# A float32 two-block transformer on one core: where the context stream's low parts are made, how many raw weight buffers it has, and in which order four matmul strips stand

## The chip, the cores and the metric

One core of a Trainium2 chip. The metric is the device time of one execution in microseconds; medians of several runs are compared. The core has five engines, which run their own instruction queues in order and wait for each other by semaphores: TensorE (PE; its weight loads are shown as PEld), VectorE (DVE), ScalarE (ACT), GpSimd (POOL) and SyncE (SP), which here issues all large DMAs.

## The reference

Two blocks after each other, all in float32, on 256 tokens of width 1024. Cut to what matters here:

```python
def first_block(x, ...):                  # "block 1"
    proj = rms_norm(x) @ w_in             # RWKV-7 columns and sparse-attention columns
    y_r = rwkv7_group(proj[..., :R_COLS], ...)   # a scan over 256 tokens, 8 heads
    y_n = nsa_group(proj[..., R_COLS:], ...)     # three kinds of attention
    h = x + concat([y_r, y_n]) @ w_out
    h = h + swiglu(rms_norm(h), ...)
    return rms_norm(h)

def second_block(x, c, ctx, c_ctx, ...):  # two layers
    for l in range(2):
        mod_x = silu(c) @ w_ada[l] + b_ada[l]        # 9216 columns, one row
        mod_c = silu(c_ctx) @ w_ada[l] + b_ada[l]    # the same weights, a second row
        h_x = half_ffn(h_x, mod_x[0:3]); h_c = half_ffn(h_c, mod_c[0:3])
        # mixer (neighbourhood attention, pooling, grouped attention), out projection, second half_ffn
    return rms_norm(h_x)
```

`h_c`, the context stream, starts from `ctx` and not from block 1, so its first feed-forward can run beside block 1.

## The kernel before, in words

A float32 product is made from three fast ones: each operand is split into a high part (rounded to the fast format) and a low part (what is left), and high x high, low x high and high x low are summed in PSUM. For the weights this is `Stream.get` (L351 to L358): a tile of 512 KB is loaded into a raw buffer (`r`, L349), ScalarE casts it to the high part (`h`, L356), and the stream's engine `self.e` subtracts to make the low part (`l`, L357). `gemm` (L360) then issues, for eight slices k, the products with `h` (L364, L365), and after them those with `l` (L368). Three numbers set a stream's depth: `nr` raw buffers and `nh` of each part.

Three streams matter. `st` in `block1` (L549, 2 raw buffers, 3 of each part) feeds block 1's projection: eight tiles in its first loop (L578 to L583), then 17 tiles of which 15 are L631's loop, then eight compression weights that are loaded raw; the first two of these go to the raw buffers and the other six straight into part buffers (L347). `st_c` (L1595, 3 raw buffers, 2 of each part, low parts on GpSimd) feeds the context stream: its feed-forward (66 tiles) and its mixer (14 tiles). `st_c` also carries the modulation weights, which are only loaded (L1162) and used raw. A third stream `s` feeds everything else, on VectorE.

The modulation (`Ada.step`, L1155) multiplies two rows (padded to 32) with 2048 columns at a time: four strips of 512 columns, which go to four groups of 32 PSUM partitions (L1168), eight slices k each. The strips of one k lie in two raw tiles, two strips each. The last part of a layer has strips of 256 columns, all four in one tile. 80 such quartets are made in all: 43 ahead of block 1's output projection, the rest during the feed-forwards of the second block's first layer.

The order of the work on each engine is set by a scheduler, which simulates the engines and picks, of the instructions that could run, the earliest in program order. Block 1 stands ahead of the context stream in the program, so the context's matmuls (output tiles `f`, inputs `yhc`, `ylc`, `hh`, `hl`) fill what block 1 leaves. The end of block 1, the RWKV part, is serial:
- Gram matrices (L951), a round trip through DRAM, 31 steps of two VectorE operations each that invert small triangles (L977, L978), a second round trip, and the products with the result (L994 to L1007);
- the chunk loop: for each of eight chunks of 32 tokens L1023, an addition on VectorE (L1024), L1031 and L1032, and an update of the state on VectorE (L1041);
- the tail: L1048, L1064, L849 with a power on GpSimd (L855), L864, L1083 and L1084, then block 1's output projection, whose first matmul is L364 with input `mixh`, at 530.70 us.

Of the kernel before, what the change touches and what calls it, by code (L numbers as in the profile page):

```python
# [15 lines left out]
OP = mybir.AluOpType  # L16
AX = mybir.AxisListType
PSUM = bass.MemoryType.PSUM
DRAM = bass.MemoryType.DRAM

D = 1024
KD = 8
# [243 lines left out]
def build(tc, A, O, dbg=(), stop=None):  # L266
    nc = tc.nc
    v, s, g, te, sy = nc.vector, nc.scalar, nc.gpsimd, nc.tensor, nc.sync
    es = ExitStack()
# [29 lines left out]
    f32 = lambda a: a.bitcast(F32)  # L299
# [31 lines left out]


    class Stream:
        def __init__(self, name, nr, nh, side=None, stack=es, eng=None, parts=None):
            self.nr = nr
            self.raw = pool(name + "r", nr, side=side, stack=stack)
            self.h = pool(name + "h", nh, side=side, stack=parts or stack)
            self.l = pool(name + "l", nh, side=side, stack=parts or stack)
            self.q = sy
            self.e = eng or v  # L340

        def load(self, src, a, b, i=0):

# [8 lines left out]
        def get(self, src, a, b):  # L352
            r = self.load(src, a, b)
            h = tl(self.h, [128, 1024], F32R, tag="h")[:, 0:a * b].rearrange("p (a b) -> p a b", a=a)
            l = tl(self.l, [128, 1024], F32R, tag="l")[:, 0:a * b].rearrange("p (a b) -> p a b", a=a)
            s.copy(h, r)  # L356
            self.e.tensor_tensor(l, r, f32(h), op=OP.subtract)  # L357
            return h, l  # L358

    def gemm(pt, w, m0, m1, xs):  # L360
# [126 lines left out]
    def block1(ps, early, ready):  # L487
# [12 lines left out]
        with tc.tile_pool(name="ropet", bufs=1) as rp:  # L500
# [8 lines left out]
            for i, ph in ((0, 0.25), (1, 0.0)):  # L509
# [4 lines left out]
                r = tl(rp, [128, 24], name="r")  # L514
# [31 lines left out]
            next(early, None)  # L546
        with ExitStack() as e:
            yp = pool("b1y", 1, stack=e)
            st = Stream("s1", 2, 3, stack=e)  # L549
            yh = tl(yp, [128, KD, T], F32R, name="yh")  # L550
            yl = tl(yp, [128, KD, T], F32R, name="yl")
            with ExitStack() as e2:
# [17 lines left out]
            for b in range(2):  # L570
                pts = [ps(512), ps(512)]
                for kp in range(4):
                    wh, wl = st.get(A["w1m"][b, kp], 2, 512)
                    for k2 in range(2):
                        k = kp * 2 + k2
# [4 lines left out]
                    for k2 in range(2):  # L580
                        k = kp * 2 + k2
                        for t in range(2):
                            te.matmul(pts[t], yh[:, k, t * 128:t * 128 + 128], wl[:, k2], start=False, stop=k == KD - 1)  # L583
                for t in range(2):
                    cos, sin = rope[:, 0, t * 8:t * 8 + 8], rope[:, 1, t * 8:t * 8 + 8]
                    if b == 0:
                        q = tl(pp, [128, 8, 64], tag="qtm", bufs=1)
# [5 lines left out]
                        for h4 in range(2):  # L593
                            pt = ps(512)
# [8 lines left out]
                    else:  # L603
# [8 lines left out]
                        pt = ps(512)  # L612
# [18 lines left out]
            for m in range(15):  # L631
                w = st.get(A["w1s"][m], 8, 128)
# [3 lines left out]
                pt = ps(T)  # L636
# [8 lines left out]
                nr = 32 if m == 14 else 128  # L645
# [17 lines left out]
            for i, (pe, nm) in enumerate((("pe_k", "k"), ("pe_v", "v"))):  # L663
                w = st.get(A["w1s"][15 + i], 8, 128)
                pt = ps(T)
# [57 lines left out]
        with ExitStack() as e:  # L723
            pp = pool("nsap", 2, stack=e)
            pcT = [None, None]
            for t in range(2):
                psc = ps(128)
                for h in range(8):
                    q = QT[:, h, t * 128:t * 128 + 128]
# [4 lines left out]
                sc = tl(pp, sh, tag="csc")  # L734
# [11 lines left out]
                pt = ps(128)  # L746
# [3 lines left out]
            for t in range(2):  # L750
                nk = 128 * (t + 1)
                po = ps(512, tag="o")
                for pr in range(4):
                    PT = []
                    for h in (2 * pr, 2 * pr + 1):
                        kv = h // 4
                        q = QT[:, h, t * 128:t * 128 + 128]
# [26 lines left out]
                    for b in range(nb + 1):  # L784
                        for j in range(2):
                            h = 2 * pr + j
                            out = po[j * 64:j * 64 + 64, pr * 128:pr * 128 + 128]
                            if b < nb:
                                w, kt = divmod(b, t + 1)
# [15 lines left out]
        with ExitStack() as e:  # L805
# [183 lines left out]
            for t in range(2):  # L989
                pw = ps(512)  # L990
                for p in range(4):
                    for j in range(2):
                        h = 2 * p + j
# [17 lines left out]
            for t in range(2):  # L1011
                py = ps(512, tag="o") if t == 0 else ps(512, tag="o")
                pyv = py.rearrange("p (a i) -> p a i", a=4)
                for q in range(4):
# [12 lines left out]
                    if c < 7:  # L1027
                        pS = ps(512)
                        for p in range(4):
                            w = slice(p * 128, p * 128 + 128)  # L1030
# [12 lines left out]
                for p in range(4):  # L1043
                    for b in range(2):
                        for j in range(2):
                            h = 2 * p + j
# [95 lines left out]
    class Ada:  # L1142
# [12 lines left out]
        def step(self, i, st, ps):  # L1155
            l, M = self.l, self.M
            src = A[f"ada{l}"]
            n = 512 if i < 4 else 256
            pt = ps(n)
            for k in range(KD):  # L1160
                if i < 4:
                    ws = [st.load(src[i * 16 + k * 2 + b].rearrange("p (a b) -> p a b", a=2), 2, 512) for b in range(2)]  # L1162
                    w = [ws[j // 2][:, j % 2] for j in range(4)]
                else:
                    ws = st.load(src[64 + k].rearrange("p (a b) -> p a b", a=4), 4, 256)
                    w = [ws[:, j] for j in range(4)]
                for j in range(4):
                    te.matmul(pt[j * 32:j * 32 + 32], adac[:, k], w[j], start=k == 0, stop=k == KD - 1)  # L1168
                if k < KD - 1:
                    yield  # L1170
            y = tl(st.pad, [128, 512], tag="ada", bufs=1)[:, 0:n]
            s.copy(y, pt)
            p2 = ps(n)
            nb = n // 128
            for b in range(nb):
                te.transpose(p2[:, b * 128:b * 128 + 128], y[:, b * 128:b * 128 + 128], ident)
            m = self.M_[:, i * 16:i * 16 + 4 * nb]
            v.tensor_copy(m.rearrange("p (j b) i -> p j b i", j=4), p2.rearrange("p (b j c) -> p j b c", b=nb, j=4)[:, :, :, 0:2])
            v.tensor_add(m, m, V(f"bada{l}")[:, i * 16:i * 16 + 4 * nb, None].to_broadcast([128, 4 * nb, 2]))
            gg = V(f"ng{l}").rearrange("p (j k) -> p j k", j=3)  # L1180
            for m in ((0, 1), (2, 3), (4, 5), (6, 7), (8,))[i]:
                if m % 3 == 1:
                    v.scalar_tensor_tensor(self.GS[:, m // 3], M[:, m], 1.0, gg[:, m // 3, :, None].to_broadcast([128, 8, 2]),
                                           op0=OP.add, op1=OP.mult)
                elif m in (2, 8):
                    v.tensor_scalar(M[:, m], M[:, m], 0.5, None, op0=OP.mult)
            yield
# [404 lines left out]

    rs, rs2 = ExitStack(), ExitStack()
    pad = pool("pada", 1, side=R, stack=rs)
    st_c = Stream("sc", 3, 2, side=R, stack=rs, eng=g, parts=rs2)  # L1595
    st_c.pad = pad
    e = ExitStack()
    first = []
# [165 lines left out]
```

## Time and profile before

| | us |
|---|---|
| median of 3 runs | 2322.16 |
| lowest, highest | 2317.82, 2325.53 |
| the profiled execution | 2317.79 |
| its span, first to last instruction | 2315.6 |
| TensorE busy in it | 2215.6 |
| VectorE, ScalarE, GpSimd busy | 1365.0, 965.7, 361.1 |

How to read it: the span is the profiled execution's own; what lies between it and 2317.79 us is around the first and the last instruction. Busy is the time in which an engine has an instruction in work. An engine's idle time matters only where another engine, on the path to the end, waits for it. In the rows below, "L1168" is a line of the kernel, `f<-r,sc` names the output and input tiles, and an arrow `<-` behind a time in brackets names what ended a wait.

### The profile page before, as it was taken

Reading aid. Unit: us, or ns where it says so; the run is one execution under the profiler, and the core shown is the slowest. Engines: PE = TensorE matmul, PEld = TensorE weight load, DVE = VectorE, ACT = ScalarE, POOL = GpSimd, SP = SyncE. Lnnn points to the kernel's source line nnn. Section 1 sums busy time; section 2 is a strip of 40 time slices with the busy share of each in tenths; the row PEclk is TensorE's granted clock in tenths of the full one; section 3 lists DMA queues with packets and bytes.
Section 4 is the critical chain, followed back from the end, with each engine's and each line's share of the span. In section 5 each row is a group of like instructions: output and inputs, shape, how many; then the busy total and the mean of one; then the engine's idle time right before and its main releaser. Section 6 shows DMA issues by size and latency. Waiting matters only on the chain.

```text
span 2315.6 us, 38336 instructions
## 1 busy us (share of the span) xinstructions
PE 2215.6 (96%) x15317; PEld 1935.3 (84%) x15317; DVE 1365.0 (59%) x2442; ACT 965.7 (42%) x1602; POOL 361.1 (16%) x286
## 2 busy tenths in 40 slices
PE   7999988998999899998999999999999999989998
PEld 3687876878999799997878777798888889878998
DVE  4465567348665876667765333357534347776665
ACT  4334432226444555445643222245332325564443
POOL 2025464444010300002010000011000002310000
PEclk9999999999999999999999999999999999999999
DMA  8765544436655245554166434376623235413554
GB/s 312 255 220 191 175 159 143 135 121 215 197 183 176 91 129 167 185 168 144 58 221 228 175 131 167 134 236 210 200 87 97 95 119 170 140 46 122 187 183 127
DMA packets 114929, 376.25 MB, mean 162 GB/s; under 512 B 18464, under 2 KB 24480, under 8 KB 114752
## 3 DMA queue, kind: packets, MB, share of 16 engines
q1 hardware_dynamic: 114752, 373.82, 49.1%
q8 instruction: 120, 1.97, 0.3%
q14 instruction: 57, 0.47, 0.1%
HBM read 372.20 MB, written 1.57 MB: 161 GB/s over the span
## 4 chain that ended last, share of the span: by engine, by line
PE 76%; issue 9%; DVE 7%; DMA 4%; POOL 2%; ACT 1%; SPq 0%; POOLq 0%; DVEq 0%; ACTq 0%
PE m L364 13%; PE m L365 13%; PE m L368 13%; PE f L364 8%; PE f L365 7%; PE f L368 7%; PE f L1168 4%; PE o L1399 2%; DVE l L357 1%; PE f L1389 1%; DMA r<-in_up 1%; ACT h L356 1%; DMA r<-in_ada 1%; DVE tm L977 1%; POOL sa L400 1%
## 5 line engine op out<-in xcount | busy, mean ns | idle before, releaser
L356 ACT CAST h<-r 128x1024 fp32r<-128x1024 f32 (+1 forms) x547 | 570.0, 1043 | 950.4 <-PE m L365 453.9
L357 DVE TENSOR_TENSOR l<-r,h 128x1024 fp32r<-128x1024 f32 (+1 forms) x467 | 575.5, 1233 | 284.1 <-ACT h L356 236.7
L365 PE MATMUL m<-yl,h 128*128 128x256 f32 (+1 forms) x1624 | 441.9, 303 | 3.5 <-DVE yl L437 3.4
L364 PE MATMUL m<-yh,h 128*128 128x256 f32 (+1 forms) x1624 | 441.5, 303 | 1.5 <-ACT yh L436 1.5
L364 PEld LDWEIGHTS m<-yh,h 128*128 128x128 f32 x1624 | 310.1, 192 | 27.3 <-issue 10.4
L365 PEld LDWEIGHTS m<-yl,h 128*128 128x128 f32 x1624 | 310.4, 192 | 21.4 <-DVE yl L437 6.4
L368 PE MATMUL m<-yh,l 128*128 128x256 f32 (+1 forms) x1624 | 258.6, 300 | 0.0
L357 POOL TENSOR_TENSOR l<-r,h 128x1024 fp32r<-128x1024 f32 x80 | 194.2, 2431 | 368.2 <-ACT h L356 234.3
L368 PEld LDWEIGHTS m<-yh,l 128*128 128x128 f32 x1624 | 225.1, 190 | 14.2 <-issue 3.7
L400 POOL TENSOR_TENSOR sa<-sa,sq 128x256 f32<-128x256 f32 x81 | 83.3, 1029 | 873.2 <-ACT sq L396 462.9
L365 PE MATMUL m<-hl,h 128*128 128x256 f32 (+1 forms) x738 | 207.0, 303 | 0.0
L364 PE MATMUL m<-hh,h 128*128 128x256 f32 (+1 forms) x738 | 197.2, 304 | 0.0
L364 PE MATMUL f<-yh,h 128*128 128x256 f32 (+1 forms) x624 | 185.3, 321 | 1.1 <-ACT yh L436 1.1
L365 PE MATMUL f<-yl,h 128*128 128x256 f32 (+1 forms) x624 | 184.1, 319 | 0.0
L365 PEld LDWEIGHTS m<-hl,h 128*128 128x128 f32 x738 | 139.8, 189 | 6.9 <-issue 0.4
L364 PEld LDWEIGHTS m<-hh,h 128*128 128x128 f32 x738 | 135.9, 189 | 11.1 <-issue 2.1
L1549 DVE SCALAR_TENSOR_TENSOR res<-m,mod,res 128x256 f32<-128x256 f32 x176 | 81.0, 479 | 108.0 <-PE m L368 105.5
L364 PEld LDWEIGHTS f<-yh,h 128*128 128x128 f32 x624 | 119.2, 191 | 17.3 <-issue 5.4
L364 PE MATMUL f<-hh,h 128*128 128x256 f32 (+1 forms) x446 | 126.6, 313 | 6.5 <-DVE res L1549 6.3
L368 PE MATMUL m<-hh,l 128*128 128x256 f32 (+1 forms) x738 | 129.9, 302 | 0.0
L365 PE MATMUL f<-hl,h 128*128 128x256 f32 (+1 forms) x446 | 126.6, 306 | 2.4 <-DVE hl L372 2.4
L1168 PE MATMUL f<-r,sc 128*32 128x512 f32 (+1 forms) x640 | 118.3, 573 | 8.4 <-DMA r<-in_ada 7.8
(513 smaller groups left out, 3772.5 us busy)
## 6 DMA issues: line engine op xcount, KB each, us to landing
r<-in_up SPq DMA_DIRECT2D x252, 512.0 KB, 3.6
r<-in_ada SPq DMA_DIRECT2D x144, 512.0 KB, 4.4
r<-in_dn SPq DMA_DIRECT2D x98, 512.0 KB, 3.9
r<-in_w1u SPq DMA_DIRECT2D x44, 512.0 KB, 3.5
r<-in_dn SPq DMA_DIRECT2D x32, 448.0 KB, 3.3
r<-in_w2m SPq DMA_DIRECT2D x24, 512.0 KB, 3.8
r<-in_w2o SPq DMA_DIRECT2D x24, 512.0 KB, 3.4
r<-in_w1d SPq DMA_DIRECT2D x22, 512.0 KB, 3.5
```

The costliest lines, as they stand in the source:

```text
L356: s.copy(h, r)
L357: self.e.tensor_tensor(l, r, f32(h), op=OP.subtract)
L364: te.matmul(pt, w[0][:, k, m0:m1], xs[k][0], start=k == 0, stop=False)
L365: te.matmul(pt, w[0][:, k, m0:m1], xs[k][1], start=False, stop=False)
L368: te.matmul(pt, w[1][:, k, m0:m1], xs[k][0], start=False, stop=k == n - 1)
L400: g.tensor_tensor(acc, acc, sq, op=OP.add)
L977: v.tensor_mul(tm, TW[:, 0:m, j:j + 1].to_broadcast([128, m, n]), Ls[:, j:j + 1, j + 1:32].to_broadcast([128, m, n]))
L1168: te.matmul(pt[j * 32:j * 32 + 32], adac[:, k], w[j], start=k == 0, stop=k == KD - 1)
L1389: te.transpose(pT[:, b * 128:b * 128 + 128], P[:, b * 128:b * 128 + 128], ident)
L1399: te.matmul(po[j * 64:j * 64 + 64], vals(b // 2, b % 2, kvof(2 * pr + j)), PT[j][:, b], start=b == 0, stop=b == nt - 1)
L1549: v.scalar_tensor_tensor(r, pt[:, i * T:i * T + T], ad[l].M[:, m, d, q:q + 1], r, op0=OP.mult, op1=OP.add)
```

## The change

Four edits. The context stream's low parts are made on VectorE, as all others are. It has four raw buffers instead of three. Block 1's stream has two buffers for each part instead of three. And the four strips of a modulation step are tied to each other in the scheduler, in the order 2, 3, 0, 1: the half that is loaded last comes first. The tie sets an order and adds no semaphore.

```diff
+NOSYNC = mybir.DependencyInfo(mybir.DependencyClass.NoSync, mybir.DependencyReason.DATA)
...
-        def __init__(self, name, nr, nh, side=None, stack=es, eng=None, parts=None):
+        def __init__(self, name, nr, nh, side=None, stack=es, parts=None):
...
-            self.e = eng or v
...
             s.copy(h, r)
-            self.e.tensor_tensor(l, r, f32(h), op=OP.subtract)
+            v.tensor_sub(l, r, f32(h))
             return h, l
...
-            st = Stream("s1", 2, 3, stack=e)
+            st = Stream("s1", 2, 2, stack=e)
...
-                for j in range(4):
-                    te.matmul(pt[j * 32:j * 32 + 32], adac[:, k], w[j], start=k == 0, stop=k == KD - 1)
+
+                last = None
+                for j in (2, 3, 0, 1):
+                    q = te.matmul(pt[j * 32:j * 32 + 32], adac[:, k], w[j], start=k == 0, stop=k == KD - 1).ins
+                    if last is not None:
+                        tc.add_manual_dep(q, last.name, NOSYNC, reason="strips side by side")
+                    last = q
...
-    st_c = Stream("sc", 3, 2, side=R, stack=rs, eng=g, parts=rs2)
+    st_c = Stream("sc", 4, 2, side=R, stack=rs, parts=rs2)
```

The diff moves far more than it names, since the scheduler draws up the whole order anew. Three places follow; a number behind a name is the tile's own, and "x2" counts equal rows. In the changed kernel, lines behind L1166 are five higher (L1168 is L1170).

TensorE, in block 1's first projection, two strips at a time, before:

```order
L578 MATMUL m_460<-h_481,yh_264 128x512
L579 MATMUL m_460<-h_481,yl_265 128x512
L1168 MATMUL f_160<-r_209,sc_82 32x512 x2
L578 MATMUL m_459<-h_481,yh_264 128x512
L579 MATMUL m_459<-h_481,yl_265 128x512
L1168 MATMUL f_160<-r_211,sc_82 32x512 x2
L578 MATMUL m_460<-h_481,yh_264 128x512
```

The same quartet (raw tiles 209 and 211) with the change:

```order
L596 MATMUL m_424<-cst_58,qhl_421 128x128 x4
L596 MATMUL m_430<-cst_58,qhl_421 128x128 x4
L1170 MATMUL f_160<-r_211,sc_82 32x512 x2
L1170 MATMUL f_160<-r_209,sc_82 32x512 x2
L596 MATMUL m_447<-cst_58,qhl_444 128x128 x4
L596 MATMUL m_453<-cst_58,qhl_444 128x128 x4
```

Its two halves now stand together, and it comes earlier, ahead of the transposes of the second token tile.

VectorE, in the chain of triangle steps (`tm`, `TW`), with the change:

```order
L978 TENSOR_TENSOR TW_2181<-TW_2181,tm_2193 128x2x29
L357 TENSOR_TENSOR l_4946<-r_4943,h_4945 128x1024
L977 TENSOR_TENSOR tm_2196<-TW_2181,Ls_2178 128x2x28
L1554 SCALAR_TENSOR_TENSOR res_60<-f_4915,mod_11_85,res_60 128x256
L978 TENSOR_TENSOR TW_2181<-TW_2181,tm_2196 128x2x28
L977 TENSOR_TENSOR tm_2199<-TW_2181,Ls_2178 128x3x27
L1554 SCALAR_TENSOR_TENSOR res_60<-f_4929,mod_11_85,res_60 128x256
L978 TENSOR_TENSOR TW_2181<-TW_2181,tm_2199 128x3x27
L357 TENSOR_TENSOR l_4952<-r_4949,h_4951 128x1024
```

Before, no L357 stood among these steps on VectorE; now eight do, from the first to the last of the 62.

TensorE, in the chunk loop, at the chunk of tile 2394, before:

```order
L1023 MATMUL m_2394<-SB_406_1913,WT_2290 32x128 x4
L1026 MATMUL o_2356<-AR_2009,SB_406_1913 128x32 x4
L1031 MATMUL m_2404<-Vt_2071,Kt_2057 128x128
L368 MATMUL f_4827<-hh_4719,l_4810 128x256
L368 MATMUL f_4827<-hh_4797,l_4810 128x256
L364 MATMUL f_4847<-hh_4562,h_4843 128x256
L365 MATMUL f_4847<-hl_4563,h_4843 128x256
L364 MATMUL f_4847<-hh_4641,h_4843 128x256
```

and with the change:

```order
L1023 MATMUL m_2394<-SB_406_1913,WT_2290 32x128 x4
L1026 MATMUL o_2356<-AR_2009,SB_406_1913 128x32 x4
L1031 MATMUL m_2404<-Vt_2071,Kt_2057 128x128
L1032 MATMUL m_2404<-U_2334,Bt_2043 128x128
L1031 MATMUL m_2404<-Vt_2071,Kt_2057 128x128
L1032 MATMUL m_2404<-U_2334,Bt_2043 128x128
L1031 MATMUL m_2404<-Vt_2071,Kt_2057 128x128
L1032 MATMUL m_2404<-U_2334,Bt_2043 128x128
L1031 MATMUL m_2404<-Vt_2071,Kt_2057 128x128
L1032 MATMUL m_2404<-U_2334,Bt_2043 128x128
L1023 MATMUL m_2419<-SB_407_1914,WT_2290 32x128 x4
```

The context matmuls (`f`) that stood between a chunk's own are gone from here: all of the context's first feed-forward now stands ahead of L994.

## Rows read from the trace of the kernel before

**Rows 1.** The page's head: the span, and TensorE's busy time.
```profile
span 2315.6 us, 38336 instructions
PE 2215.6 (96%) x15317; PEld 1935.3 (84%) x15317; DVE 1365.0 (59%) x2442; ACT 965.7 (42%) x1602; POOL 361.1 (16%) x286
```

**Rows 2.** Windows: length, busy us (instructions) by engine, granted clock, DMA share, GB/s.
```profile
10.00:72.00 62.00, 50.70 (x209) 25.11 (x209) 31.80 (x77) 24.20 (x45) 8.11 (x9) 0.93 0.85 309
72.00:292.00 220.00, 214.49 (x1657) 175.11 (x1655) 119.30 (x251) 88.27 (x184) 79.68 (x54) 1.00 0.62 207
...
371.00:423.00 52.00, 40.62 (x302) 37.30 (x301) 37.65 (x85) 13.53 (x18) 23.96 (x10) 0.90 0.48 139
423.00:503.00 80.00, 80.00 (x679) 70.92 (x676) 25.05 (x44) 18.14 (x25) 35.85 (x24) 1.00 0.36 118
503.00:531.00 28.00, 20.70 (x123) 12.25 (x122) 19.16 (x35) 9.22 (x19) 14.98 (x13) 0.93 0.58 209
...
1240.00:1740.00 500.00, 500.00 (x2911) 413.49 (x2910) 235.00 (x348) 166.37 (x224) 20.02 (x18) 1.00 0.51 170
```

**Rows 3.** Timeline of TensorE at modulation strips: start, us, what, count.
```profile
31.20 1.05 PE L1168 MATMUL f<-r,sc 128*32 128x512 f32 x4
32.19 0.96 PE L583 MATMUL m<-l,yh 128*128 128x512 f32 x3
...
1270.81 1.07 PE L1168 MATMUL f<-r,sc 128*32 128x512 f32 x8
```

**Rows 4.** Groups by line and shape: low parts on VectorE and GpSimd, busy us, mean ns.
```profile
L357 DVE TENSOR_TENSOR l<-r,h 128x1024 fp32r<-128x1024 f32 x435 | 540.9, 1244 | 268.3 <-ACT h L356 225.9 <-PE m L368 24.3 <-PE f L368 3.9
L357 POOL TENSOR_TENSOR l<-r,h 128x1024 fp32r<-128x1024 f32 x80 | 194.2, 2431 | 368.2 <-ACT h L356 234.3 <-PE f L1274 94.4 <-PE f L368 33.7
```

**Rows 5.** Timeline of VectorE: triangle steps, first, two in the middle, last.
```profile
374.01 1.07 DVE L977 TENSOR_TENSOR tm<-TW,Ls 128x31 f32<-128x31 f32 x1 [0.72 <-DMA TW<-in_cst]
...
380.35 2.04 DVE L978 TENSOR_TENSOR TW<-TW,tm 128x115 f32<-128x115 f32 x1
382.43 0.28 DVE L977 TENSOR_TENSOR tm<-TW,Ls 128x110 f32<-128x110 f32 x1
...
411.28 0.19 DVE L978 TENSOR_TENSOR TW<-TW,tm 128x16 f32<-128x16 f32 x1
```

**Rows 6.** Timeline of GpSimd at the stretched step of rows 5.
```profile
379.86 2.40 POOL L357 TENSOR_TENSOR l<-r,h 128x1024 fp32r<-128x1024 f32 x1 [4.83 <-ACT h L356]
```

**Rows 7.** Timeline of TensorE: two waits for VectorE, in brackets.
```profile
303.60 0.39 PE L365 MATMUL f<-hl,h 128*128 128x256 f32 x1 [2.41 <-DVE hl L372]
...
390.40 0.57 PE L364 MATMUL f<-hh,h 128*128 128x256 f32 x1 [4.17 <-DVE res L1549]
```

**Rows 8.** Timeline of TensorE: L994, then one chunk of the chunk loop.
```profile
423.14 1.09 PE L994 MATMUL m<-TT,At 128*64 128x128 f32 x16
...
468.17 1.06 PE L1023 MATMUL m<-SB,WT 128*32 128x128 f32 x8
...
473.20 0.48 PE L1032 MATMUL m<-U,Bt 32*128 32x128 f32 x2
...
476.61 1.12 PE L368 MATMUL f<-yhc,l 128*128 128x256 f32 x8
477.57 0.28 PE L364 MATMUL f<-yhc,h 128*128 128x256 f32 x1
...
478.50 1.06 PE L1023 MATMUL m<-SB,WT 128*32 128x128 f32 x8
```

**Rows 9.** Timeline of VectorE in the same chunk: the update of the state.
```profile
475.13 0.87 DVE L1041 TENSOR_TENSOR SB<-st,m 64x256 f32<-64x256 f32 x2 [3.33 <-PE m L1032]
```

**Rows 10.** The chain of waits in the tail, in order of time.
```profile
511.77 2.91 POOL hr L855
...
523.36 6.14 DMA r<-in_w1o
```

**Rows 11.** Timeline of TensorE: a wait for modulation weights.
```profile
69.80 1.92 PE L1168 MATMUL f<-r,sc 128*32 128x512 f32 x4 [2.58 <-DMA r<-in_ada]
```

## The prediction

> **What bounds the kernel now.** I read the totals first. TensorE is busy for 2215.6 of 2315.6 us [rows 1], so the time can fall in two ways only: less work on TensorE, or less of the 100 us in which it waits. The windows by stage say where these are [rows 2]. From 10 to 72 us TensorE works 50.70 of 62 us beside DMA engines at a share of 0.85; from 371 to 423 us it works 40.62 of 52; from 423 to 503 us it never waits; from 503 to 531 us it works 20.70 of 28. From 1240 to 1740 us it is full. So the change can bite in the first 531 us, up to the first matmul of block 1's output projection, and beyond that only through work that TensorE loses.
>
> The third view is TensorE's timeline at the modulation matmuls [rows 3]. A piece of two strips (x4, since each strip is two passes) takes 1.05 us, and all four strips side by side (x8) take 1.07. The next matmul starts 0.99 us after the beginning of the former. So a cut quartet costs a whole further piece, whatever is in it.
>
> The fourth view is VectorE against GpSimd. The low part takes 1.24 us on VectorE and 2.43 us on GpSimd [rows 4]. But GpSimd does not work for nothing: in the chain of 31 steps that inverts the small triangles a step of 0.28 us takes 2.04 us where it meets a low part on GpSimd, here the one that starts at 379.86 us [rows 5, 6]. The chain runs from 374.01 to 411.28 us, and seven of its 62 operations are stretched like this. TensorE's waits in that region are for VectorE: 2.41 us for the low part of an activation, 4.17 us for a residual sum [rows 7].
>
> The last views are the chunk loop and the tail [rows 8 to 10]. A chunk starts every 10.33 us (468.17 to 478.50), but its own steps are short, and context matmuls fill the rest. In the tail the chain goes through GpSimd's power (2.91 us), and then through a weight load that starts only after block 1's last matmul and lands 6.14 us later.
>
> **The change part by part.** *Tied strips.* Counted quartet by quartet in the order, there are 60 pieces of 512 columns and 10 of 256 ahead of 531 us before, and 39 and 9 with the change; behind 531 us 35 wide ones become 31 and the 10 narrow ones stay. (Nine of 80 quartets stay cut.) 21 x 0.99 + 0.57 (the narrow piece; an estimate from the wide one, a little over half) = 21.4 us less ahead of 531 us, 4 x 0.99 = 4.0 us less behind it. **25 us** of TensorE's work go. The pieces behind 531 us stand in full stretches, so those 4 us are safe.
>
> *Low parts to VectorE.* 80 x 1.24 = 99 us more on VectorE, 194.2 us less on GpSimd. VectorE has room on average (37.65 of 52 us in its densest window), and it gets back what the collisions cost. I summed, over all VectorE operations that ran beside a GpSimd low part, what each took beyond the shortest of its kind: 59 us in 40 operations, of which rows 5 shows one. So VectorE's net load is +40 us over some 650 us. Of TensorE's waits, those of rows 7 and their neighbours are the ones that it can remove; I credit 3 us ahead of the triangles.
>
> *Fourth raw buffer.* TensorE waits for the modulation weights up to 72 us (2.58 us at the worst [rows 11], 11.3 us of idle time in all in that window). The DMA engines are at 0.85 there, so at most 15% of 62 us, 9 us, can come. With a buffer more, both weights of a quartet and a next one can be under way. The low end is nothing, if tying makes a quartet wait for its later half. I take 5 us, the middle, and 2 us for the clock, which is granted at 0.93 over this window.
>
> *Two part buffers in block 1's projection.* TensorE is busy 214.49 of 220 us from 72 to 292 us, which hides casts and low parts that come a buffer later: nothing. If the cover goes, the price is the two compression weights that must now wait for a buffer, at most two landings like the 6.14 us of rows 10, 12 us. A gain is excluded, since fewer buffers start nothing earlier.
>
> *What the order moves.* This is the large term on the other side. Context matmuls issued before the first Gram matmul (L951): 982 before, 1344 with the change. Between the last Gram matmul and the triangles' result (L994): 265, now 192. From there to the end of the chunk loop: 254, now none. In the tail: 42, now none. The work is the same, but it is spent early, and block 1's serial end runs bare.
> - 371 to 423 us. Before, 52 us with 11.4 idle. The chain loses seven collisions of about 2.1 us (14.7), gains eight low parts of 1.2 us among its steps (9.8), and waits some 3 us for the last context group: 37.3 - 14.7 + 9.8 + 3 = 35.4, and with the 14.7 us of DMA round trips around it (52 - 37.3) 50 us. TensorE has 192 x 0.12 + seven quartets, 29 us. Idle 21 instead of 11.4: **+10**. A matmul of 0.12 us is the pitch of rows 8 (0.96 us for eight).
> - Chunk loop. 80 us, all busy. Of these 254 x 0.12 + four small quartets = 33 us are context. Bare, a chunk is TensorE's 1.06 (L1023) + 1.06 (L1026, as many passes) + 0.4 (a first L1031) + 1.9 (from the first L1032 at 473.20 to VectorE's update at 475.13), then the update's 0.87: 5.3 us [rows 8, 9]. Six of these, an opening of 13 and a last part of 5 make 50 us; own work is 43 to 47. **+5**, and 10 at the worst.
> - Tail. 28 us with 7.3 idle; 42 x 0.12 + 4.9 + 0.6 = 10 us of context work leave it, of which only some 4 lay in the chain's way (the pieces ahead of the last L1084 delay the load of rows 10). 24 us with 10 of work: idle 14, **+7**.
> [...]
>
> **The sum.** -25 (strips) - 3 (collisions) - 7 (early loads and clock) + 10 + 5 + 7 + 3 = -10; I round the bare stretches up by 2 us, because a chain worked out from its steps leaves small handovers out: **-8 us**. The profiled execution took 2317.79 us (span 2315.6 and 2.2 around it), 4.4 us under the median of the runs shown, 2322.16. The sum was made against the former; laid on the median it gives **2314 us**.
>
> **The rivals.** *A: most of the strips' gain stays.* If the context work that was pulled ahead runs in time that TensorE wasted before, and VectorE without collisions shortens block 1 itself by more than I credit, the bare stretches cost 10 us instead of 25: 2322 - 25 = 2297 us. For it: 59 us of stretched VectorE operations [rows 5]. Against: TensorE is at 214.49 of 220 us where most of that work lands, so little time is wasted there.
>
> *B: nothing measurable.* The early loads are bound by DMA bandwidth, tying only shifts the wait, and collisions gave TensorE no time: -25 + 25 + 2 = +2, 2324 us. For it: the DMA share of 0.85 to 72 us.
>
> *C: slower, by the bare chunk loop at half clock.* In the loop as it will be, TensorE stops about 1 us in every 5. If that lets the granted clock fall to 0.5, each chunk's 4.3 us of matmuls take 4.3 us more; seven chunks at half clock throughout are 30 us. It decides from about half of the loop on: -8 + 15 = +7, 2329 us; throughout, 2344. For it: the three windows of rows 2 that hold waits of over 2 us have 0.93, 0.90 and 0.93. Against: the window from 72 to 292 us also has 5.5 us of idle time in it, and 1.00. [...]
>
> *That the change does not do what it says:* the order shows the quartets joined and the low parts on VectorE; so I give it nothing.
>
> **How the numbers follow.** My forecast 0.35, A 0.25, B 0.25, C 0.15. A measurement of this kernel tells about 0.3%, 7 us, from no change. The forecast lies just over that edge and is split 0.20 faster, 0.15 same. Faster 0.20 + 0.25 = 0.45, same 0.15 + 0.25 = 0.40, slower 0.15. The range has A's 2297 at its low end (less 1) and reaches up to C's lower price, 2329, with 3 us for the compression weights: 2296 to 2332. The two tails hold about 0.2.
>
> **What the profile will show.** Right: modulation matmuls in runs of x8 of 1.07 us; no low part on GpSimd, and no triangle step over 0.5 us; L994 after a wait of TensorE of 15 us or more; chunks every 5 to 6 us; the output projection's first matmul at 518 to 528 us, and from there on the same distance to the end, less 4 us. Wrong: the first output matmul at 505 us (A), or after 530 us with a clock of 0.5 in the chunk loop (C), or TensorE's idle time up to 72 us unchanged (B).

## The result and the profile after

The changed kernel takes 2339.85 us (median of 4 runs, 2337.22 to 2344.43) against 2323.27 us for the kernel before (now four runs): 1.0077 times the time before, with a 95% interval of 1.0051 to 1.0103. It is slower, by 17 us. The forecast was 2314 us in a range of 2296 to 2332 us; of the rivals, C, the bare chunk loop at half clock, comes closest. The profiled execution took 2344.43 us, 4.6 us above the median, so a few us in its rows are chance.

The head of the profile's page of the changed kernel (span, then busy time by engine), to be laid beside [rows 1]:

```profile
span 2342.6 us, 38319 instructions
PE 2223.6 (95%) x15317; PEld 1960.2 (84%) x15317; DVE 1385.1 (59%) x2522; ACT 964.8 (41%) x1602; POOL 165.2 (7%) x206
```

TensorE is busy for 8 us more with the same number of matmuls, though 26 pieces of strips were to leave it. The windows by stage of the changed kernel say where that is (columns as in [rows 2]; the stages begin at the first Gram matmul 377, the last 396, L994 444, the first chunk 467, the end of L1048 526, the first output matmul 556):

```profile
10.00:72.00 62.00, 50.25 (x231) 28.81 (x232) 30.41 (x76) 23.38 (x44) 6.68 (x9) 0.87 0.92 336
...
72.00:377.00 305.00, 297.76 (x2374) 255.49 (x2373) 198.42 (x389) 130.82 (x244) 11.20 (x25) 0.99 0.60 217
377.00:396.00 19.00, 19.00 (x114) 13.88 (x112) 14.99 (x39) 2.95 (x4) 1.91 (x2) 1.00 0.38 98
396.00:444.00 48.00, 30.48 (x251) 24.86 (x250) 32.63 (x95) 10.17 (x13) 0.00 (x0) 0.84 0.65 222
444.00:467.00 23.00, 21.63 (x112) 20.47 (x112) 2.64 (x5) 2.34 (x4) 0.45 (x1) 0.50 0.04 6
467.00:526.00 59.00, 53.31 (x272) 46.15 (x272) 10.40 (x20) 0.58 (x1) 6.93 (x12) 0.53 0.00 1
526.00:556.00 30.00, 19.78 (x54) 11.11 (x53) 13.89 (x25) 7.64 (x16) 10.35 (x11) 0.56 0.14 49
1265.00:1765.00 500.00, 499.96 (x2952) 416.11 (x2951) 236.58 (x352) 167.77 (x227) 19.24 (x18) 1.00 0.49 173
```

From 444 to 556 us the granted clock is 0.50 to 0.56, nearly all of it at 0.5, the lower of the two levels that both traces' records of the granted clock hold (0.5 and 1.0); before, the same work stood at 1.00 and in the tail at 0.93 [rows 2]. TensorE is busy for 95 of these 112 us, with 438 matmuls, against 802 in 108 us before. TensorE's timeline of the changed kernel shows how it began, and one chunk (waits in brackets):

```profile
428.62 1.94 PE L1170 MATMUL f<-r,sc 128*32 128x512 f32 x8 [3.95 <-DMA r<-in_ada]
444.38 1.97 PE L994 MATMUL m<-TT,At 128*64 128x128 f32 x16 [13.83 <-DMA TT<-d_t]
...
467.07 1.89 PE L1023 MATMUL m<-SB,WT 128*32 128x128 f32 x8 [1.06 <-DVE SB L1037]
468.89 1.92 PE L1026 MATMUL o<-AR,SB 128*128 128x32 f32 x8
...
471.32 0.63 PE L1032 MATMUL m<-U,Bt 32*128 32x128 f32 x2
...
475.64 1.89 PE L1023 MATMUL m<-SB,WT 128*32 128x128 f32 x8 [1.12 <-DVE SB L1041]
...
555.57 0.58 PE L364 MATMUL m<-mixh,h 128*128 128x256 f32 x1 [0.39 <-ACT h L356]
```

The context's last matmul ended at 422.6 us, and the strips ahead of L994 at 430.6 us. After waits of 3.95 and 13.83 us, L994's 16 passes take 1.97 us instead of 1.09 [rows 8], L1023 1.89 instead of 1.06, and a chunk 8.57 us (467.07 to 475.64), of which 1.12 us are a wait.

To find the difference I summed, for each matmul in both traces, the distance from its start to the next one's, less the wait that the trace names, by kind; "own" is everything that is neither context feed-forward nor strip:

| stretch, us | length | own | context | strips | waits | at clock 0.5 |
|---|---|---|---|---|---|---|
| start to first Gram, before | 348.3 | 126.8 | 130.3 | 57.1 | 34.1 | 17.1 |
| the same, after | 377.1 | 132.1 | 172.6 | 43.5 | 29.0 | 20.5 |
| Gram to L994, before | 74.8 | 14.2 | 44.5 | 4.8 | 11.4 | 10.2 |
| the same, after | 67.3 | 11.8 | 31.5 | 6.0 | 17.9 | 15.9 |
| L994 to end of L1048, before | 79.1 | 42.3 | 34.0 | 2.9 | 0 | 0 |
| the same, after | 81.3 | 74.7 | 0 | 0 | 6.7 | 78.0 |
| tail, before | 28.5 | 10.0 | 5.8 | 5.4 | 7.3 | 3.7 |
| the same, after | 29.8 | 19.6 | 0 | 0 | 10.2 | 26.4 |
| output projection to the end, before | 1784.9 | 1527.2 | 169.6 | 40.3 | 40.5 | 64.6 |
| the same, after | 1787.0 | 1524.1 | 170.8 | 36.3 | 48.5 | 59.9 |

The strips gave what was counted: 20.7 us less ahead of the output projection, 4.0 us behind it. The output projection begins 24.9 us later all the same. Over the four stretches ahead of it, own matmuls take 44.9 us more, waits 11.0 us more, strips 20.7 us less, and the same context matmuls 10.5 us less. Between L994 and the output projection alone, the same own matmuls take 94.3 instead of 52.3 us. **These 42 us more than eat the strips' gain.** 48 us of context and strips left this stretch, and its length did not fall. Whether the clock is the cause or only came with it, the experiments had to show.

### The profile page after: what moved, and what is told of

It reads as the page before. It is cut to its first block, busy times and chain, and to the rows that moved or that the text cites. A ratio compares the mean times of both kernels' runs of the same rounds, so it can differ in the third digit from the quotient of the medians.

```text
span 2342.6 us, 38319 instructions
## 1 busy us (share of the span) xinstructions
PE 2223.6 (95%) x15317; PEld 1960.2 (84%) x15317; DVE 1385.1 (59%) x2522; ACT 964.8 (41%) x1602; POOL 165.2 (7%) x206
## 3 DMA queue, kind: packets, MB, share of 16 engines
q8 instruction: 120, 1.97, 0.3%
## 4 chain that ended last, share of the span: by engine, by line
PE 78%; issue 9%; DMA 5%; DVE 5%; POOL 1%; ACT 1%; SPq 0%; POOLq 0%; DVEq 0%; ACTq 0%
PE m L364 13%; PE m L365 13%; PE m L368 13%; PE f L364 8%; PE f L368 7%; PE f L365 7%; PE f L1170 3%; DMA r<-in_ada 2%; PE o L1404 2%; DVE l L357 1%; PE f L1394 1%; ACT h L356 1%; PE f L1274 1%; PE f L1275 1%; PE m L1031 1%
## 5 line engine op out<-in xcount | busy, mean ns | idle before, releaser
L357 DVE TENSOR_TENSOR l<-r,h 128x1024 fp32r<-128x1024 f32 (+1 forms) x547 | 666.9, 1220 | 312.8 <-ACT h L356 274.6
L365 PEld LDWEIGHTS f<-yl,h 128*128 128x128 f32 x624 | 118.8, 190 | 7.8
L368 PEld LDWEIGHTS m<-hh,l 128*128 128x128 f32 x738 | 109.0, 190 | 6.3 <-issue 0.4
```

Source lines behind the costliest of these rows:

```text
L357: v.tensor_sub(l, r, f32(h))
L365: te.matmul(pt, w[0][:, k, m0:m1], xs[k][1], start=False, stop=False)
L368: te.matmul(pt, w[1][:, k, m0:m1], xs[k][0], start=False, stop=k == n - 1)
```

## The experiments

Theory 1: the bare end of block 1 runs at half clock, and that is the loss. Theory 2: context work that was pulled ahead delays block 1, and the bare chain is long by itself; the clock is a symptom. The expectations name further theories where they are first needed. A run's kernel may have its lines shifted by some numbers; where that is so, the text says which line is meant. Ratios are to the kernel before, run on the same chip, with the 95% interval.

**The strips tied, alone.** The change's fourth edit, the strips' order and tie, on the kernel before.

> The kernel before with the tied strips alone (three raw buffers, low parts on GpSimd, three part buffers). The order keeps 195 context matmuls in the chunk loop and 149 in the tail, and has 89 pieces of strips instead of 115. Theory 1 (the half clock of the bare chunk loop ate the gain of the strips): the fill is there, so the clock stays at 1.00 in the loop, a chunk takes about 10 us as before, and the strips' 25 us are gained: 2300 us (2294 to 2306). Theory 2 (the context work that was pulled ahead delays block 1, the clock has no share): 2300 us too, since less work, 884 matmuls, stands ahead of the first Gram matmul. Theory 3 (the strips side by side gain nothing): 2320 to 2326 us.

2327.48 against 2322.41 us, 1.0017 (1.0005 to 1.003): nothing gained. Theories 1 and 2, which both asked for 2300 us, missed, and it lies 1.5 us above theory 3's range. Windows of this run: the stretch up to the Gram matmuls, the chunk loop, the tail.

```profile
17.00:342.00 325.00, 287.87 (x2058) 236.09 (x2059) 188.50 (x353) 126.69 (x248) 106.07 (x70) 0.93 0.59 204
426.00:483.00 57.00, 57.00 (x459) 49.44 (x458) 22.10 (x33) 11.55 (x16) 26.25 (x19) 1.00 0.33 112
488.00:521.00 33.00, 31.43 (x224) 25.12 (x220) 19.46 (x31) 11.83 (x17) 20.38 (x10) 1.00 0.43 142
```

The loop keeps its clock, as theory 1 said. The strips did get shorter, by 26.2 us over the whole run (the same sums as in the table: 110.5 before, 84.3 here). But TensorE's waits rose from 93.3 to 114.6 us, and its time at 0.5 from 96 to 129 us; the stretch up to the Gram matmuls has 0.93. So what the strips saved turned into waits, above all ahead of the Gram matmuls, where TensorE waited some 50 instead of 34 us, longest for the modulation weights' loads (9.7 us) and for casts of the context's weights (7.3 us). 36 context matmuls and 20 strips also fell behind the output projection.

**The changed kernel, context work held back by order.** Two versions (the second also puts L994 behind its 72nd tile); a hold is a dependence that sets the order and adds no semaphore:

```diff
+HOLD = lambda i: "g" if 50 <= i < 62 else min((i - 62) // 2, 6) if i >= 62 else None
...
+                tc.add_manual_dep(q, marks[m].name, NOSYNC, reason="held for the chunk loop")
```

> The changed kernel whole, but context tiles from the 50th on are held, by order alone, until the last Gram matmul, and from the 62nd on until chunk after chunk: 217 context matmuls in the chunk loop, 167 in the tail, 912 ahead of the first Gram matmul. Theory 1 (half clock in the bare loop): clock 1.00 in the loop, 2296 to 2306 us. Theory 2 (work pulled ahead delays block 1): the same. Theory 4 (the low parts on VectorE slow block 1's serial end): the low parts are still on VectorE and now stand in the loop, so no faster than 2330 us.

2323.28 against 2322.41 us, 1.0003 (0.9992 to 1.0014): a miss too, 17 us above theory 1's range and below theory 4's.

> The changed kernel with another split of the same context work: tiles from the 58th on are held until the last Gram matmul, from the 72nd on until chunk after chunk, and L994 stands behind the 72nd. By the order 1080 matmuls ahead of the first Gram matmul, 264 ahead of L994, 181 in the chunk loop, 18 in the tail. Theory 1b: clock 1.00 from L994 to the end of the loop, block 1's own matmuls there 28 us instead of 48; less waiting ahead of the Gram matmuls than with 912 (the run with tiles held from the 50th): 2304 to 2316 us, below the kernel before. Theory 7 (what the strips save only turns into waits of TensorE, whatever the order): 2318 to 2326 us.

2328.30 against 2320.60 us, 1.0036 (1.0021 to 1.0051), a miss of both ranges. Windows, of the first version from L994 on and in the loop, then of the second:

```profile
401.00:428.00 27.00, 27.00 (x139) 25.75 (x140) 3.13 (x6) 3.11 (x5) 1.24 (x2) 0.51 0.03 5
428.00:487.00 59.00, 59.00 (x480) 51.76 (x477) 26.44 (x43) 13.10 (x19) 6.19 (x10) 1.00 0.36 117
```

```profile
419.00:445.00 26.00, 25.96 (x135) 24.78 (x135) 3.13 (x6) 2.50 (x5) 1.23 (x2) 0.52 0.02 3
445.00:501.00 56.00, 56.00 (x444) 49.07 (x444) 25.70 (x42) 10.58 (x14) 6.18 (x10) 0.97 0.31 106
```

With context work back in the loop the clock is back (1.00 and 0.97), and own matmuls there take 27.6 us in the first version (47.6 without), with the low parts still on VectorE: theory 4 falls for the loop. But the work from L994 to the first chunk stayed bare and at 0.51 and 0.52, and the holds made TensorE wait 40.5 and 32.2 us between the first projection matmul and the first Gram matmul, where the changed kernel waits 16.8. Context work only goes round so far: what fills one stretch is missing in another.

**The stops filled with matmuls of no use.** On the changed kernel, 20 behind each chunk's last L1032, where TensorE waits for VectorE (1.12 us ahead of L1023 at 475.64 us above), and in a second run 200 more behind the context's last tile; their results go nowhere, and the next chunk's L1023 stands behind them:

```diff
+            def idle(n, q):
+                pt = ps(128)
+                for i in range(n):
+                    r = te.matmul(pt, identr, identr, start=i == 0, stop=i == n - 1).ins
+                    tc.add_manual_dep(r, q.name, NOSYNC, reason="idle")
+                    q = r
+                return q
```

> The changed kernel with 20 matmuls of 128x128 that nobody reads behind each chunk's last state matmul, where TensorE waits about 1.1 us for VectorE. Nothing else is moved. Theory 1: with the short stops filled, the granted clock comes back to 1.00 within the loop, a chunk takes 5.5 to 6.5 us instead of 8.57, and the whole 2318 to 2328 us. Theory 2 (the clock has no share in the time, the chain is long by itself): each of seven chunks becomes longer by what of the 20 matmuls does not fit into 1.1 us, 0.5 to 1.5 us each, 2343 to 2350 us.

> The same 20 matmuls a chunk, and 200 more ahead of L994, where TensorE waits for the triangles. Theory 1: the clock never falls, so the Gram-to-chunk part and all chunks run at 1.00; a chunk 5.5 to 6.5 us; 2310 to 2322 us, below the run with the loop's matmuls alone. Theory 2: 2343 to 2355 us.

2360.68 us, 1.0162 (1.013 to 1.0193), and 2346.84 us, 1.0099 (1.0073 to 1.0125). The second is in theory 2's range, the first 11 us above it. The first run's timeline of TensorE (there L1042 is the changed kernel's L1032, L1031 its L1023, L1013 the filler) and its window over the loop:

```profile
482.64 0.63 PE L1042 MATMUL m<-U,Bt 32*128 32x128 f32 x2
483.20 4.53 PE L1013 MATMUL m<-identr 128*128 128x128 f32 x20
487.66 1.92 PE L1031 MATMUL m<-SB,WT 128*32 128x128 f32 x8
```

```profile
464.00:538.00 74.00, 74.00 (x353) 67.15 (x352) 9.70 (x19) 0.59 (x1) 6.18 (x10) 0.52 0.00 1
```

TensorE no longer waits at all, and the clock is 0.52. The second run entered the loop at 1.00 (its window from 438 to 455 us) and fell in it to a mean of 0.65:

```profile
438.00:455.00 17.00, 17.00 (x160) 14.28 (x160) 3.12 (x8) 2.34 (x4) 1.24 (x2) 1.00 0.28 94
455.00:520.00 65.00, 63.36 (x357) 57.02 (x353) 12.06 (x21) 2.68 (x3) 6.18 (x10) 0.65 0.12 41
```

So the stops are not what keeps the clock down, and since the clock stayed low, these runs don't tell what it costs. Theory 1b: it is matmuls like the context's that bring it back.

**The same places filled with matmuls of the context's kind**, 128x512 in the fast format (the context's own are 128x256): 10 a chunk, then also 60 ahead of L994. They differ from the first fillers in more than width: they stream block 1's data, where those streamed the identity against itself.

```diff
+                wide = b1mix[0][:, 4:6].rearrange("p a t -> p (a t)")
...
+                    r = te.matmul(pt, identr, wide, start=i == 0, stop=i == n - 1).ins
```

> The changed kernel with 10 matmuls of 128x512 in the fast format, of the context's kind, that nobody reads, behind each chunk's last state matmul; nothing else is moved. Theory 1b (the clock is what the bare end costs, and it is matmuls like the context's that bring it back, not the mere absence of waits): the granted clock rises to 1.00 within the first chunks, a chunk takes 6.5 to 7.5 us (4.3 of its own and 2.2 to 2.6 of these) instead of 8.57, and the whole 2325 to 2336 us although 70 matmuls were added. Theory 2 (a chain that is long by itself): a chunk 8.57 + 1 to 2 us, the whole 2345 to 2356 us.

> The same, and 60 more such matmuls ahead of L994, in the wait for the triangles. Theory 1b: clock 1.00 from the last Gram matmul to the end of the loop; the part from L994 to the first chunk 17 us instead of 22.7, a chunk 6.5 to 7.5 us; 2318 to 2330 us. Theory 2: 2345 to 2360 us.

2334.72 us, 1.0061 (1.004 to 1.0081), and 2315.50 us, 0.9983 (0.997 to 0.9996), both as theory 1b said, the second below its range. Windows of the first over L994 to the loop and over the loop; then windows of the second over the same, and one chunk in its timeline (L1038 is the changed kernel's L1023, L1043 its L1026, L1020 the filler):

```profile
443.00:469.00 26.00, 26.00 (x123) 23.42 (x121) 2.64 (x5) 2.34 (x4) 1.23 (x2) 0.50 0.02 3
469.00:514.00 45.00, 45.00 (x292) 37.06 (x290) 9.61 (x19) 0.58 (x1) 6.17 (x10) 0.92 0.00 1
```

```profile
432.00:447.00 15.00, 15.00 (x132) 12.77 (x129) 4.91 (x7) 4.27 (x6) 1.24 (x2) 1.00 0.78 268
447.00:492.00 45.00, 45.00 (x292) 37.07 (x290) 9.61 (x19) 0.58 (x1) 6.17 (x10) 0.92 0.02 6
```

```profile
446.86 1.06 PE L1038 MATMUL m<-SB,WT 128*32 128x128 f32 x8
447.85 1.08 PE L1043 MATMUL o<-AR,SB 128*128 128x32 f32 x8
...
450.83 2.59 PE L1020 MATMUL m<-mixh,identr 128*128 128x512 f32 x10
453.36 1.06 PE L1038 MATMUL m<-SB,WT 128*32 128x128 f32 x8
```

This chunk takes 6.50 us with 2.53 us of useless work in it, instead of 8.57; the mean of the six distances is 7.36 instead of 8.62, since the granted clock over the loop is 0.92 and matmuls of L1048 stand in it. **Work was only added, and by the two ratios the second run is some 22 us faster than the changed kernel.** Not all of that is the clock's. In the second run a quartet of strips and two low parts also moved behind the fillers, and the triangle steps take 30.7 us instead of 36.4 with six low parts among them instead of eight; that is about 6 us. The first run is the clean one. TensorE's order up to the output projection is the changed kernel's with the fillers put in (four matmuls of L1048 change places with a group of them), and from the first chunk to the first output matmul it takes 76.0 us instead of 88.5, with 70 matmuls more. So in the loop, at 0.92 instead of 0.53, the clock is the cause. From L994 to the first chunk the second run points the same way: 15.1 us at a clock of 1.00, with a quartet and 10 fillers more, instead of 22.7 at 0.50. Theory 2's second half, that the bare chain is long by itself, falls. The first run's whole time doesn't show it: its interval overlaps the changed kernel's. Theory 2's first half is true as far as it goes, since the Gram matmuls come 28.8 us later; but that is work that had stood in the later stretches.

**Which edit emptied the loop.** The fourth raw buffer with the two part buffers, then the low parts on VectorE, each alone on the kernel before; and the change without the low parts.

```diff
...
-    st_c = Stream("sc", 3, 2, side=R, stack=rs, eng=g, parts=rs2)
+    st_c = Stream("sc", 4, 2, side=R, stack=rs, eng=g, parts=rs2)
```

> The kernel before with the fourth raw buffer and block 1's two part buffers alone (untied strips, low parts on GpSimd). By the order 1178 context matmuls stand ahead of the first Gram matmul instead of 982, 46 and 15 strips are left in the chunk loop, none in the tail. Theory 1b: the tail and part of the chunk loop run at 0.5, 10 to 20 us are lost there and 196 x 0.12 = 24 us come earlier, of which little is gained ahead: 2325 to 2340 us. Theory 5 (a fourth raw buffer costs nothing, it only starts loads earlier): 2316 to 2324 us.

> The kernel before with the context's low parts on VectorE alone. By the order 1125 context matmuls ahead of the first Gram matmul, 24 and 12 strips left in the chunk loop, none in the tail. Theory 1b: half clock in loop and tail, 2330 to 2345 us. Theory 6 (without collisions VectorE's chain gets shorter by some 15 us and nothing is lost): 2308 to 2318 us.

> The change without its first edit: low parts of the context back on GpSimd, four raw buffers, two part buffers, tied strips. By the order 1128 context matmuls ahead of the first Gram matmul, 268 ahead of L994, 104 and 24 strips in the chunk loop, none in the tail. Theory 1b: the loop keeps most of its clock, the tail runs at 0.5; 2310 to 2324 us. Theory 4 (the low parts on VectorE cost nothing by themselves): as the whole change, 2335 to 2345 us.

2327.25 us, 1.0018 (1.0003 to 1.0033); 2338.85 us, 1.0074 (1.0049 to 1.0098); 2310.60 us, 0.9957 (0.9943 to 0.9972). The third beats both kernels. Loop windows of the first, the second and the third:

```profile
453.00:503.00 50.00, 47.16 (x323) 38.90 (x322) 16.34 (x32) 4.40 (x6) 13.19 (x13) 0.81 0.34 117
```

```profile
472.00:530.00 58.00, 53.42 (x292) 43.64 (x290) 16.33 (x32) 3.05 (x4) 7.39 (x12) 0.62 0.25 82
```

```profile
441.00:490.00 49.00, 47.65 (x384) 39.03 (x384) 18.81 (x35) 7.38 (x10) 17.23 (x15) 0.98 0.40 143
```

The kernel before has 210 context matmuls in the loop at a clock of 1.00. With 46 context matmuls and 15 strips left the clock is 0.81, with 24 and 12 (by the order) it is 0.62, with 104 and 24 it is 0.98. So the raw buffer and the low parts on VectorE each empty most of the loop, and VectorE's edit alone costs what the whole change costs. Not all of that need be the clock's: in its trace, which is 18 us above the run's median, 12 low parts stand among the triangle steps, and these take 44.8 us instead of 37.3. How much of the loss is VectorE's time and how much the emptied loop was not tried apart.

**The change without the tie**, and **the two part buffers alone**.

> The changed kernel without its last edit: strips untied. The order is nearly the same as with it (1323 context matmuls ahead of the first Gram matmul, 218 ahead of L994, none in loop and tail), but strips stand in 57 pieces ahead of the output projection and 45 behind it, instead of 48 and 41. Theory 1b (strips save TensorE's time where it is full, and in this order it is full ahead of the Gram matmuls): 9 to 13 us over the changed kernel, 2348 to 2354 us. Theory 7 (what the strips save turns into waits): as the changed kernel, 2337 to 2343 us.

> The kernel before with two part buffers in block 1's projection instead of three, alone. The order keeps the same counts in each stretch. As the prediction had it, nothing: 2317 to 2326 us; if the two compression weights that must wait for a buffer are on the path, up to 12 us more, 2334 us.

2342.50 us, 1.0091 (1.0073 to 1.011), theory 7's figure: 13 pieces that should be worth 13 us show 3 us over the changed kernel's median, and the two intervals overlap. And 2318.83 us, 0.9989 (0.9975 to 1.0003): the part buffers cost nothing.

**The bare end filled with useful work.** The changed kernel with 24 quartets of the second layer's modulation let loose behind the context's feed-forward, and two combinations.

```diff
-        fill(max(0, 40 - 8 * len(EARLY) - done[0]))
+        fill(max(0, 64 - 8 * len(EARLY) - done[0]))
```

> The changed kernel with 24 more modulation quartets (of the second layer) let loose behind the context's feed-forward, so that they may fill the bare end: by the order 9 pieces in the chunk loop and 8 in the tail, 24 pieces fewer behind the output projection. Theory 1b: the quartets' 24 us leave full stretches and stand in waits; whether four strips a chunk bring the clock back is open: 2316 us if they don't (2340 - 24), 2300 us if they do. Theory 2: 2316 us.

> Both: context tiles held from the 60th and the 75th on, and modulation quartets of the second layer let loose: 169 context matmuls in the chunk loop, 8 quartets in the tail, 6 pieces fewer behind the output projection. Theory 1b: 2300 to 2312 us, a few us below the run that only holds. Theory 7: 2318 to 2326 us.

> The change without its first edit, and 24 modulation quartets of the second layer let loose behind the context's feed-forward: by the order 104 context matmuls and 28 strips in the chunk loop, 32 strips in the tail, 8 wide and 2 narrow pieces fewer behind the output projection. Theory 1b: 2310.6 less 9 us of pieces, less up to 8 us of clock in the tail: 2293 to 2303 us. Theory 2 (no share of the clock): 2302 us.

2299.22 us (2292.26 to 2312.4), 0.9916 (0.9892 to 0.9939); 2312.94 us, 0.9968 (0.9952 to 0.9983); 2308.48 us, 0.995 (0.9932 to 0.9968), a miss by 5 us; the second lies 1 us above its range. The first is the fastest of all, 21 us under the kernel before and by the two ratios 37 under the changed one. Its windows from L994 to the loop and over the loop, and one chunk:

```profile
441.00:459.00 18.00, 18.00 (x140) 12.82 (x137) 3.51 (x8) 2.92 (x5) 1.24 (x2) 0.88 0.48 174
459.00:500.00 41.00, 39.44 (x313) 27.39 (x309) 10.33 (x23) 1.17 (x2) 6.16 (x10) 0.96 0.71 256
```

```profile
459.03 1.07 PE L1023 MATMUL m<-SB,WT 128*32 128x128 f32 x8
...
463.02 1.06 PE L1170 MATMUL f<-r,sc 128*32 128x512 f32 x8
464.21 1.03 PE L1023 MATMUL m<-SB,WT 128*32 128x128 f32 x8
```

One quartet stands in the stop, the clock is 0.96, and this chunk takes 5.18 us; the mean of the six distances, with nine quartets in them, is 6.49. The DMA engines, idle in the changed kernel's loop (share 0.00), work at 0.71. From the first output matmul (532.19 us) to the end it takes 27 us less than the changed kernel (1759.6 against 1787.0); its strips there take 11.6 instead of 36.3 us, so those pieces left full stretches. The combinations gain less; that their stretches held other work already is the likely reason, not one that was tried.

## Why the prediction was wrong

- **Strips: the work right, the time wrong.** 25 us of TensorE's work were forecast to go, 24.7 went. That all of it would come as time was wrong: tied alone they gave nothing, and untied in the changed kernel they cost about 3 us of 13, within the noise. Not even the 4 us behind the output projection show: the distance from its first matmul to the end is 1787.0 us against 1784.9, with 8 us more of waits, and these runs don't tell whether that is chance.
- **Collisions: right, in part by luck.** No triangle step is stretched (the longest takes 0.30 us, against 2.04 us in [rows 5]); the chain of 31 steps takes 36.4 us (398.88 to 435.29 us in VectorE's timeline) for 35.4 forecast, and 37.3 before. But with the same edit it took 30.7 us in the run with fillers ahead of L994 (six low parts among the steps) and 44.8 us where the edit stood alone (twelve), so the forecast hung on how many the order puts there.
- **Fourth raw buffer and early clock: wrong.** 7 us were credited. From 10 to 72 us TensorE is busy for 50.25 instead of 50.70 us, at 0.87 instead of 0.93, with the DMA share up from 0.85 to 0.92 (309 to 336 GB/s). With the raw buffer and the two part buffers alone it is 51.55 us at 0.94, share 0.90. So more was loaded and TensorE gained at most 1 us there. That bandwidth sets this stretch, as rival B had it, fits, but was not tried by itself. Over the whole stretch up to the first Gram matmul the waits did fall by 5 us (34.1 to 29.0); which edit did that is open.
- **Part buffers: right**, by the run with that edit alone.
- **Waits of the bare stretches: right in kind.** 22 us were forecast for the three stretches; by the table they rose from 18.7 to 34.8 us, by 16, and all waits up to the output projection by 11 (52.8 to 63.8). L994 came after waits of 3.95 and 13.83 us; 15 or more was forecast.
- **The step that failed: the clock, put at +3.** No row and no run shows this term; it was the author's estimate of what the matmuls behind the bare wait ahead of L994 would lose, and the chunks were put at 5.3 us [rows 8, 9], the pace of matmuls at 1.00. What the runs showed in its place: behind that wait of 13.83 us the clock stayed at 0.5 for 104 of the 111 us up to the output projection, and own matmuls took 42 us more. Where the clock stood at 0.96 the forecast of a chunk was good: 5.18 us for the chunk shown of the version with the quartets. Replace 8.57 by 5.3 for seven chunks (23 us) and the 22.7 us from L994 to the first chunk by the 15.1 us of the run with fillers in both places (8 us), and the output projection begins at 525 us, inside the 518 to 528 us forecast, and the whole takes 2309 us, by an estimate from these rows.
- **Rival C was right in its result (2344 us, half clock throughout) and wrong in its reason.** The run took 2339.85 us. C's number owes something to luck: it charged 4.3 us for each of seven chunks, 30 us, where 8.57 less 5.3 us make 23, and beyond the forecast's +3 nothing for the stretches ahead of the loop and behind it, which lost clock too. It blamed the short stops and asked whether they let the clock fall. The stops could be filled and the clock stayed down: the loop without any stop ran at 0.52, so the stops were not needed for the low clock. The argument against C, that a stretch with waits of 5.5 us in 220 stood at 1.00, compared stretches whose matmuls differ.

## What to carry to other kernels

In this kernel, matmuls from another stream that stood in a serial stretch did two things: they used its waits, and TensorE's clock was up for the stretch's own small matmuls (in the chunk loop 1.00 with 210 context matmuls and 0.53 with none; L1023 took 1.06 and 1.89 us). An edit that lets that stream finish earlier can cost the second without gaining the first, as this one did; count, in the order, what is left in each serial stretch, and if it is nothing, price that stretch also at the half clock measured here (0.50 to 0.56). If nothing can be held back, bring later work that needs no result forward into it, here weights' products that were due much later (0.96 in the loop, and 21 us under the kernel before).

## What the runs showed of the hardware that was not expected

- With 20 fillers of 128x128 a chunk TensorE never waited and was still near half clock: 0.52 over 74 us with a busy share of 1.00, when all its matmuls were the loop's small ones and 128x128 ones, nearly each with its weight load (67.15 of 74 us of weight loading). In the second run with them the granted clock fell even after a stretch at 1.00 (0.65 on average from 455 to 520 us).
- In the same loop 10 matmuls of 128x512 a chunk gave 0.92, entered at 0.50 or at 1.00. Nine quartets of strips in the loop gave 0.96, entered from a stretch at 0.88. Fillers, strips and context matmuls differ in shape, number and data, and what of this counts these runs don't settle.
- From 0.5 to 1.0 the rows of the loop's own matmuls become shorter by less than half: L1023 1.89 to 1.06 us, L1032 0.63 to 0.38 us for two passes. From start to start the gain is larger: L1023 to the next group takes 1.82 us (467.07 to 468.89) and 0.99 us (446.86 to 447.85).
